# The weighted sums of an attention stage: one fp32 product per block in place of two float16 products

## The chip, the core and the metric

The kernel runs on one core of a Trainium2 chip. The metric is the device time of one execution in microseconds (us); lower is better. The core's engines are named as the profile names them: PE is the tensor engine, PEld its weight loads, DVE the vector engine, ACT the scalar engine, POOL the GpSimd engine, SP the queue that issues most DMAs. Work goes to each engine as a queue in program order.

## What is computed

One layer of a streaming encoder for 1024 tokens of width 1024: an input projection, three groups of heads (stick-breaking attention, a matrix-memory group, a gated group), an output projection, a mixture of 32 experts and a final gate. The change lies in the stick-breaking attention: 6 heads of width 64, blocks of 128 queries.

```python
def stick_breaking_attention(q, k, v):
    for n in range(S // 128):
        t0, kend = n * 128, n * 128 + 128
        z = einsum('bthd,bshd->bhts', q[:, t0:kend], k[:, :kend]) * scale
        log_1m = where(mask, -softplus(z), 0.0)
        after = cumsum(log_1m, axis=3, reverse=True) - log_1m
        a = where(mask, exp(log_sigmoid(z) + after), 0.0)
        outs.append(einsum('bhts,bshd->bthd', a, v[:, :kend]))   # the weighted sums
```

## The kernel before

Float32 results are made from float16 products: a number is split into a high float16 part and a low one (the rest), and a product is the sum of two or three float16 products. `split` (L138 to L140) makes the two parts: ACT copies the high part, DVE subtracts it and writes the low one. `mm3` (L142 to L145) is the three-product form of the projections.

**First part (up to about 106 us).** The input is normalised and turned, and the values are projected into `V`, which holds for each of 8 token blocks and 6 heads a high and a low float16 part of 64 columns beside each other. `values_out` (L364) writes it with `split`.

**The attention stage (about 106 to 400 us).** A hand-written order of slots: 48 steps, one per head and query block; head after head, and in each head the query blocks in the order 0, 7, 1, 6, 2, 5, 3, 4, so that short and long steps alternate. A step with query block i has i+1 blocks of 128 keys; over all steps that is 6 x 36 = 216 blocks. Each slot s runs one stage of several steps and, in between, half-groups of the remaining input projections on PE (`todo`), and side work of the gated and matrix-memory groups on DVE, ACT and POOL (`advance`). The stages of one step, in the slots in which they come:

- `scores` (slot s): PE multiplies queries and keys into a score bank of PSUM.
- `sigmoids` (s+1): ACT writes two sigmoids of the scores, `rest` and `a`.
- `products` (s+2): DVE scans `rest` backwards (L666), POOL multiplies it into `a` (L667). `a` is float32.
- `turned` (s+3): PE transposes each 128x128 block of `a` into one of two PSUM banks, "5" and "6" (L676).
- `high` and `low` (s+4): ACT copies the transposed weights as float16 (`ah`, L683); later in the slot DVE subtracts `ah` from the same PSUM bank and writes the rest as float16 (`al`, L689). A bank is free again when both have read it.
- `values` (s+5): for each block PE multiplies `ah` with high and low values side by side (128 columns, L695) and `al` with the high values (64 columns, L697), all summed in PSUM bank "7", of which there is one.
- `finish` (s+6): DVE adds the two halves of that bank into `ya` (L701). It is the first attention work of its slot on DVE; `values` of the step behind it waits until it has emptied bank "7".

The lines of a slot:

```python
            stage(s - 6, "finish")
            stage(s - 4, "high")
            stage(s - 1, "sigmoids")
            stage(s - 2, "products")
            stage(s - 4, "low")
            advance()
            # half a group of projections on PE, then:
            stage(s - 5, "values")
            # the rest of the slot's projections, then turned (s - 3) and scores (s)
```

**Behind the stage** come the chunks of the matrix memory, the output projection, the router and the experts, whose weights are loaded on SP once the arena that held the turned input is free, which is when the last projection of the stage (`pvb`) has read it.

Of the kernel before, what the change touches and what calls it, by code (L numbers as in the profile page):

```python
# [10 lines left out]
F32 = mybir.dt.float32  # L11
F16 = mybir.dt.float16
I32 = mybir.dt.int32
AF = mybir.ActivationFunctionType
OP = mybir.AluOpType
AX = mybir.AxisListType
# [3 lines left out]
P = 128  # L20
S = 1024
D = 1024
NT = S // P
# [3 lines left out]
ISW = 1.0 / SW  # L27
HA = 6
DA = 64
WA = HA * DA  # L30
# [64 lines left out]
def hybrid_kernel(ctx, tc, x, p, norm1_g, w_in, conv_w, conv_b, igate_b, fgate_b, mnorm_g, sb_out_g,  # L95
# [3 lines left out]
    nc = tc.nc  # L99
    dbg = dbg or {}  # L100

    def pool(c, name, bufs=1, side="left", space=None):
        kw = {"space": space} if space is not None else {"side": side, "reuse_waits": "tile"}
        return c.enter_context(tc.tile_pool(name=name, bufs=bufs, **kw))
# [8 lines left out]
    def bank(which, name, dt=F32, n=512):  # L113
        i = turn.get(which, 0)
        turn[which] = i + 1
        b = which[i % len(which)]
        return ps.tile([P, n], dt, tag="b" + b, name=name)
# [5 lines left out]
    def rows(src, n):  # L123
        return bass.AP(tensor=src.tensor, offset=src.offset, ap=[[0, P], [1, n]])
# [8 lines left out]
    def rnorm(src, n, name, tag):  # L133
        ms = small.tile([P, 1], F32, name=name, tag=tag + "m")
        nc.scalar.activation(jk[:, :n], src, AF.Square, accum_out=ms)
        return rsq(ms, 1, n, name, tag)

    def split(hi, lo, src, scale):  # L138
        nc.scalar.activation(hi, src, AF.Copy, scale=scale)  # L139
        nc.vector.scalar_tensor_tensor(lo, src, scale, hi, op0=OP.mult, op1=OP.subtract)  # L140
# [140 lines left out]
    ya = yap.tile([P, NT, WA], F32, name="ya")  # L281
# [9 lines left out]
    qkp = pool(cA, "qkp", 1, "right")  # L291
    at = pool(cA, "at", 2, "right")
    vp = pool(cA, "vp", 1, "right")
    V = vp.tile([P, NT, HA, 2, DA], F16, name="V")

    rests = {w: vp.tile([P, w + 1], F32, name=f"rest{w}") for w in (512, S)}
    for w in rests:
# [34 lines left out]
    with ExitStack() as cx:  # L332
        xp = pool(cx, "xp", 3, "right")
        g1 = xp.tile([P, D], F32, name="g1", bufs=1)
        vrow = xp.tile([64, P], F32, name="vrow", bufs=1)
        nc.vector.memset(vrow, 0.0)
        xs, rs = {}, {}

        def load(t):
            xs[t] = xp.tile([P, D], F32, name=f"x{t}", tag="x")  # L340
            nc.sync.dma_start(xs[t], x[0, t * P:(t + 1) * P, :])

        def root(t):
            rs[t] = rnorm(xs[t], D, f"r1_{t}", "n1")

        def norm(t):
            nc.vector.scalar_tensor_tensor(xs[t], xs[t], rs[t], g1, op0=OP.mult, op1=OP.mult)

        def turned(t):
            sl = slice(t * P, t * P + P)  # L350
            pts = []
            for k0 in (0, 4):
                pt = bank("56", f"pt{t}{k0}")
                for k in range(4):
                    nc.tensor.transpose(pt[:, k * P:(k + 1) * P], xs[t][:, (k0 + k) * P:(k0 + k + 1) * P], ident)
                pts.append((k0, pt.rearrange("p (k t) -> p k t", t=P)))
            for k0, pt in pts:
                split(hTh[:, k0:k0 + 4, sl], hTl[:, k0:k0 + 4, sl], pt, 1.0)

        def values(t):  # L360
            *_, pz = projN(f"pv{t}", WV, WA, t)
            return pz

        def values_out(t, pz):  # L364
            split(V[:, t, :, 0, :], V[:, t, :, 1, :], pz[:, :WA].rearrange("p (h d) -> p h d", d=DA), ISW)

        loads = [(vrow[16:40], conv_w[0].rearrange("j (k c) -> (j k) c", c=P)),
                 (vrow[40:46], conv_b[0].rearrange("(k c) -> k c", c=P)), (vrow[46:50], sgu_b[0]),
                 (gy[:, 0:WA], rows(sb_out_g, WA)), (gy[:, WA:WA + WM], rows(mnorm_g, WM)),
                 (gy[:, WA + WM:], rows(sgu_out_g, WU)),  # L370
                 (lgb[:, 0], rows(sgu_ln_g, WU)), (lgb[:, 1], rows(sgu_ln_b, WU))]

        def others_turned():
            pv = bank("56", "pvec")
            nc.tensor.transpose(pv[:, :64], vrow, ident[:64, :64])
            nc.vector.tensor_copy(vec, pv[:, :64])
            pt = bank("56", "psw")
            for g in range(NG):
                nc.tensor.transpose(pt[:, g * P:(g + 1) * P], sw[:, g, :], ident)
            nc.vector.tensor_copy(swT, pt.rearrange("p (g t) -> p g t", t=P))  # L380

        sw = xp.tile([P, NG, P], F32, name="sw", bufs=1)
        load(0)
        nc.scalar.dma_start(g1, rows(norm1_g, D))
        with tc.manual_schedule(engines=FOUR):
            awake(48)
            WV = load_w("wv", [(CVA, WA)], "wst4")
            load(1)
            root(0)
            norm(0)  # L390
            turned(0)
            for _ in split_w(WV):
                pass
            load(2)
            root(1)
            norm(1)
            W0 = load_w("w0", [(CQA, P), (CKA, P)], "wst4")
            sp = split_w(W0)
            for t in range(NT):
                if t + 2 < NT:  # L400
                    root(t + 2)
                pz = values(t)
                if t + 1 < NT:
                    turned(t + 1)
                if t + 2 < NT:
                    norm(t + 2)
                values_out(t, pz)
                if t + 3 < NT:
                    load(t + 3)
                for _ in range(2 if t == 2 else t < 2):  # L410
                    next(sp)
                if 0 < t < 5:
                    if t == 1:
                        nc.gpsimd.dma_start(vrow[50:58], ple_norm_g[0].rearrange("(k c) -> k c", c=P))
                    for o, src in loads[2 * t - 2:2 * t]:
                        nc.gpsimd.dma_start(o, src)
                if t == 3:
                    nc.gpsimd.dma_start(sw, sgu_w[0].rearrange("g t s -> t g s"))
                    nc.vector.memset(sw[0:64, :, 64:128], 0.0)
                    for _ in sp:  # L420
                        pass
                if t == 6:
                    others_turned()
                if t % 4 == 3:
                    for mms, then in proj_qk(0, W0, QKS[0], t // 4):
                        *_, pz = mms
                        for _ in then(pz):
                            pass
# [204 lines left out]
    class Step:  # L633
# [42 lines left out]
                    nc.tensor.transpose(pt[:, b * P:(b + 1) * P], self.a[:, (s0 + b) * P:(s0 + b + 1) * P], ident)  # L676
                self.t.append((m, pt))

        def high(self):
            self.hl = []  # L680
            for s, (m, pt) in enumerate(self.t):
                ah = at.tile([P, 512], F16, name=f"ah{self.h}{self.i}{s}", tag="ah", bufs=3)
                nc.scalar.activation(ah[:, :m * P], pt[:, :m * P], AF.Copy)  # L683
                self.hl.append(ah)

        def low(self):
            for s, (m, pt) in enumerate(self.t):
                al = at.tile([P, 512], F16, name=f"al{self.h}{self.i}{s}", tag="al", bufs=3)
                nc.vector.tensor_tensor(al[:, :m * P], pt[:, :m * P], self.hl[s][:, :m * P], op=OP.subtract)  # L689
                self.hl[s] = [(self.hl[s][:, b * P:(b + 1) * P], al[:, b * P:(b + 1) * P]) for b in range(m)]  # L690

        def values(self):
            self.pa = bank("7", f"av{self.h}{self.i}")[:, :P].rearrange("p (l d) -> p l d", l=2)
            for sb, (ah, al) in enumerate(sum(self.hl, [])):
                nc.tensor.matmul(self.pa.rearrange("p l d -> p (l d)"), ah,  # L695
                                 V[:, sb, self.h].rearrange("p l d -> p (l d)"), start=(sb == 0), stop=False)
                nc.tensor.matmul(self.pa[:, 0, :], al, V[:, sb, self.h, 0, :], start=False, stop=(sb == self.i))  # L697

        def finish(self):
            h, i = self.h, self.i  # L700
            nc.vector.tensor_reduce(ya[:, i, h * DA:(h + 1) * DA], self.pa.rearrange("p l d -> p d l"),  # L701
                                    axis=AX.X, op=OP.add)
            if h == HA - 1:
                side.append(self.norm())

# [353 lines left out]
    with tc.manual_schedule(engines=FOUR):  # L1059
# [5 lines left out]
        def stage(s, *fns):  # L1065
            if 0 <= s < NS:
                for f in fns:
                    getattr(steps[s], f)()

        m2, wo = None, w_out_all()  # L1070
        for s in range(NSLOT + 2):
# [22 lines left out]
            fresh.clear()  # L1094
            advance(quick)
            stage(s - 6, "finish")
            stage(s - 4, "high")
            stage(s - 1, "sigmoids")
            stage(s - 2, "products")
            stage(s - 4, "low")  # L1100
            advance()
            want = min(NJ, NJ * (s + 1) // NSLOT)
            if done < want:
# [825 lines left out]
```

## Time and profile before

| | us |
|---|---|
| device time, median of 3 runs (lowest to highest) | 1066.91 (1065.41 to 1067.37) |
| profiled execution, its own time | 1063.69 |
| profiled execution, span from first to last instruction | 1061.8 |
| PE busy in the span | 931.5 (88%) |
| DVE busy | 741.1 (70%) |
| ACT busy | 574.9 (54%) |
| POOL busy | 425.5 (40%) |

The span is the stretch between the first and the last instruction; the profiled execution's own time is 1.9 us more, and 3.2 us under the median. Busy shares are means over stages with different limits, so the stage of the change is read by itself. The duration shown for a matmul reaches to its modelled end, and matmuls overlap in the pipeline; what a chain of matmuls costs is read from start to start.

### The profile page before, as it was taken

Reading aid. Unit: us, or ns where it says so; the run is one execution under the profiler, and the core shown is the slowest. Engines: PE = TensorE matmul, PEld = TensorE weight load, DVE = VectorE, ACT = ScalarE, POOL = GpSimd, SP = SyncE. Lnnn points to the kernel's source line nnn. Section 1 sums busy time; section 2 is a strip of 40 time slices with the busy share of each in tenths; the row PEclk is TensorE's granted clock in tenths of the full one; section 3 lists DMA queues with packets and bytes.
Section 4 is the critical chain, followed back from the end, with each engine's and each line's share of the span. In section 5 each row is a group of like instructions: output and inputs, shape, how many; then the busy total and the mean of one; then the engine's idle time right before and its main releaser. Section 6 shows DMA issues by size and latency. Waiting matters only on the chain. (4 is left out here: it accounts for less than half of the span.)

```text
span 1061.8 us, 15986 instructions
## 1 busy us (share of the span) xinstructions
PE 931.5 (88%) x5927; PEld 538.3 (51%) x5928; DVE 741.1 (70%) x1259; ACT 574.9 (54%) x937; POOL 425.5 (40%) x383
## 2 busy tenths in 40 slices
PE   7899989988999878998887659998899899999795
PEld 4457855544665455555444434543454454445343
DVE  4454549999957965578888649897677777686333
ACT  4344555535557543333333358997676767585422
POOL 2101214565542453132333637844355445561431
PEclk8999989999999997999988789999999999999898
DMA  6411122112320277955358589999989898896330
GB/s 219 130 43 32 38 55 56 35 63 79 112 66 18 90 221 199 297 176 172 104 179 278 203 278 299 284 324 319 295 271 329 253 328 278 295 311 205 81 86 40
DMA packets 128465, 189.54 MB, mean 179 GB/s; under 512 B 13505, under 2 KB 104223, under 8 KB 128384
## 3 DMA queue, kind: packets, MB, share of 16 engines
q1 hardware_dynamic: 113376, 154.40, 45.0%
q0 software_dynamic: 14864, 33.57, 11.6%
q8 instruction: 47, 0.77, 0.3%
q10 hardware_dynamic: 144, 0.52, 0.1%
q14 instruction: 34, 0.28, 0.1%
HBM read 166.01 MB, written 37.31 MB: 191 GB/s over the span
## 5 line engine op out<-in xcount | busy, mean ns | idle before, releaser
L667 POOL TENSOR_TENSOR a<-a,rest 128x128 f32<-128x128 f32 (+7 forms) x48 | 60.7, 1264 | 169.9 <-DVE rest L666 129.0
L1269 POOL DMA_INDIRECT h2s<-yo,tabs x32 | 72.0, 2251 | 72.2 <-issue 25.2
L143 PE MATMUL pg<-arena,xT 128*128 128x512 f16 x256 | 97.8, 382 | 0.7 <-ACT xT L1231 0.7
L145 PE MATMUL pg<-arena,xT 128*128 128x512 f16 x256 | 97.6, 381 | 0.0
L144 PE MATMUL pg<-arena,xT 128*128 128x512 f16 x256 | 97.6, 381 | 0.0
L140 DVE SCALAR_TENSOR_TENSOR arena<-arena 128x2048 f16<-128x2048 f32 (+1 forms) x39 | 81.2, 2096 | 18.4 <-ACT arena L139 18.4
L666 DVE TENSOR_TENSOR_SCAN rest<-rest,one 128x128 f32<-128x128 f32 (+7 forms) x48 | 73.8, 1538 | 7.0 <-ACT rest L659 6.7
L140 DVE SCALAR_TENSOR_TENSOR arena<-ws,arena 128x2048 f16<-128x2048 f32 x29 | 66.0, 2289 | 16.7 <-ACT arena L139 16.6
L145 PEld LDWEIGHTS <-arena 128*128 128x128 f16 x516 | 51.8, 100 | 50.2 <-DVE arena L251 6.5
L144 PEld LDWEIGHTS <-arena 128*128 128x128 f16 x516 | 51.7, 100 | 39.1 <-issue 10.9
L143 PEld LDWEIGHTS <-arena 128*128 128x128 f16 x516 | 52.3, 101 | 37.1 <-issue 4.9
L139 ACT ACTIVATE arena<-arena 128x2048 f16<-128x2048 f32 (+1 forms) x39 | 67.1, 1738 | 0.4 <-DMA arena<-in_w_up_dram 0.4
L139 ACT ACTIVATE arena<-ws 128x2048 f16<-128x2048 f32 x29 | 55.3, 1925 | 2.6 <-DMA ws<-in_w_up_dram 2.6
L683 ACT ACTIVATE ah<-at 128x512 f16<-128x512 f32 (+3 forms) x72 | 32.6, 488 | 37.1 <-PE at L676 36.6
L144 PE MATMUL pd<-dl,hT 128*128 128x512 f16 x120 | 47.6, 397 | 5.2 <-DVE dl L140 5.1
L143 PE MATMUL pd<-dh,hT 128*128 128x512 f16 x120 | 47.6, 397 | 3.4 <-ACT yo L1266 3.3
L143 PE MATMUL po<-woh,yT 128*128 128x512 f16 x128 | 50.3, 393 | 0.0
L144 PE MATMUL po<-wol,yT 128*128 128x512 f16 x128 | 50.3, 393 | 0.0
L145 PE MATMUL po<-woh,yT 128*128 128x512 f16 x128 | 49.9, 390 | 0.0
L689 DVE TENSOR_TENSOR al<-at,ah 128x512 f16<-128x512 f32 (+3 forms) x72 | 36.9, 540 | 17.9 <-ACT ah L683 17.9
L140 DVE SCALAR_TENSOR_TENSOR dl<-arena,dh 128x2048 f16<-128x2048 f32 x17 | 38.9, 2289 | 13.9 <-ACT dh L139 13.9
L145 PE MATMUL pd<-dh,hT 128*128 128x512 f16 x120 | 47.3, 394 | 0.0
(661 smaller groups left out, 2715.3 us busy)
## 6 DMA issues: line engine op xcount, KB each, us to landing
arena<-in_w_down_dram SPq DMA_DIRECT2D x19, 1024.0 KB, 11.8
arena<-in_w_up_dram SPq DMA_DIRECT2D x18, 1024.0 KB, 8.0
arena<-in_w_gate_dram SPq DMA_DIRECT2D x17, 1024.0 KB, 9.4
ws<-in_w_gate_dram SPq DMA_DIRECT2D x14, 1024.0 KB, 10.2
ws<-in_w_up_dram SPq DMA_DIRECT2D x13, 1024.0 KB, 12.9
ws<-in_w_down_dram SPq DMA_DIRECT2D x12, 1024.0 KB, 8.1
arena<-in_w_in_dram SPq DMA_DIRECT2D x16, 384.0 KB, 3.1
x<-in_x_dram SPq DMA_DIRECT2D x8, 512.0 KB, 6.3
```

What stands on the lines that cost most here:

```text
L139: nc.scalar.activation(hi, src, AF.Copy, scale=scale)
L140: nc.vector.scalar_tensor_tensor(lo, src, scale, hi, op0=OP.mult, op1=OP.subtract)
L143: nc.tensor.matmul(o, a[0], w[0], start=first, stop=False)
L144: nc.tensor.matmul(o, a[0], w[1], start=False, stop=False)
L145: nc.tensor.matmul(o, a[1], w[0], start=False, stop=last)
L666: nc.vector.tensor_tensor_scan(back, back, one1.to_broadcast([P, n]), 1.0, op0=OP.mult, op1=OP.mult)
L667: nc.gpsimd.tensor_tensor(self.a[:, :n], self.a[:, :n], self.rest[:, w - n + 1:w + 1], op=OP.mult)
L683: nc.scalar.activation(ah[:, :m * P], pt[:, :m * P], AF.Copy)
L689: nc.vector.tensor_tensor(al[:, :m * P], pt[:, :m * P], self.hl[s][:, :m * P], op=OP.subtract)
L1269: return nc.gpsimd.indirect_dma_start(out=h2s, out_offset=bass.IndirectOffsetOnAxis(ap=self.tb[:, 1:2], axis=0), in_=self.yo, in_offset=No ...
```

## The change

The weights and the values stay in float32. `V` becomes one float32 tile of the same number of bytes, written by ACT alone. `high` becomes `copied`, which writes the transposed weights as float32 (`aT`); `low` is gone. `values` is one float32 matmul of 64 columns per block in place of two float16 matmuls of 128 and 64 columns, and `finish` is a copy in place of a sum of two halves.

```diff
-    V = vp.tile([P, NT, HA, 2, DA], F16, name="V")
+    V = vp.tile([P, NT, HA, DA], F32, name="V")
...
         def values_out(t, pz):
-            split(V[:, t, :, 0, :], V[:, t, :, 1, :], pz[:, :WA].rearrange("p (h d) -> p h d", d=DA), ISW)
+            nc.scalar.activation(V[:, t], pz[:, :WA].rearrange("p (h d) -> p h d", d=DA), AF.Copy, scale=ISW)
...
-        def high(self):
-            self.hl = []
+        def copied(self):
+            self.aT = []
             for s, (m, pt) in enumerate(self.t):
-                ah = at.tile([P, 512], F16, name=f"ah{self.h}{self.i}{s}", tag="ah", bufs=3)
-                nc.scalar.activation(ah[:, :m * P], pt[:, :m * P], AF.Copy)
-                self.hl.append(ah)
-
-        def low(self):
-            for s, (m, pt) in enumerate(self.t):
-                al = at.tile([P, 512], F16, name=f"al{self.h}{self.i}{s}", tag="al", bufs=3)
-                nc.vector.tensor_tensor(al[:, :m * P], pt[:, :m * P], self.hl[s][:, :m * P], op=OP.subtract)
-                self.hl[s] = [(self.hl[s][:, b * P:(b + 1) * P], al[:, b * P:(b + 1) * P]) for b in range(m)]
+                aT = at.tile([P, 512], F32, name=f"aT{self.h}{self.i}{s}", tag="aT", bufs=3)
+                nc.scalar.activation(aT[:, :m * P], pt[:, :m * P], AF.Copy)
+                self.aT += [aT[:, b * P:(b + 1) * P] for b in range(m)]

         def values(self):
-            self.pa = bank("7", f"av{self.h}{self.i}")[:, :P].rearrange("p (l d) -> p l d", l=2)
-            for sb, (ah, al) in enumerate(sum(self.hl, [])):
-                nc.tensor.matmul(self.pa.rearrange("p l d -> p (l d)"), ah,
-                                 V[:, sb, self.h].rearrange("p l d -> p (l d)"), start=(sb == 0), stop=False)
-                nc.tensor.matmul(self.pa[:, 0, :], al, V[:, sb, self.h, 0, :], start=False, stop=(sb == self.i))
+            self.pa = bank("7", f"av{self.h}{self.i}")[:, :DA]
+            for sb, aT in enumerate(self.aT):
+                nc.tensor.matmul(self.pa, aT, V[:, sb, self.h], start=(sb == 0), stop=(sb == self.i))

         def finish(self):
             h, i = self.h, self.i
-            nc.vector.tensor_reduce(ya[:, i, h * DA:(h + 1) * DA], self.pa.rearrange("p l d -> p d l"),
-                                    axis=AX.X, op=OP.add)
+            nc.vector.tensor_copy(ya[:, i, h * DA:(h + 1) * DA], self.pa)
...
             stage(s - 6, "finish")
-            stage(s - 4, "high")
+            stage(s - 4, "copied")
             stage(s - 1, "sigmoids")
             stage(s - 2, "products")
-            stage(s - 4, "low")
             advance()
```

## Rows read from the trace of the kernel before

**Rows 1.** The page's line of busy time: for each engine busy us, share of the span, instructions.

```profile
PE 931.5 (88%) x5927; PEld 538.3 (51%) x5928; DVE 741.1 (70%) x1259; ACT 574.9 (54%) x937; POOL 425.5 (40%) x383
```

**Rows 2.** The attention stage in seven stretches: from and to, length, then busy us and instructions of PE, PEld, DVE, ACT and POOL, the granted clock of PE as a share of full speed, the DMA share and GB/s.

```profile
106.00:148.50 42.50, 42.50 (x387) 34.18 (x385) 20.47 (x30) 24.17 (x50) 9.00 (x7) 1.00 0.21 53
148.50:161.00 12.50, 8.74 (x43) 4.46 (x42) 5.24 (x16) 6.89 (x14) 1.66 (x2) 0.73 0.10 23
161.00:196.00 35.00, 33.93 (x235) 20.21 (x234) 32.37 (x83) 19.18 (x45) 18.18 (x17) 1.00 0.18 46
196.00:270.50 74.50, 64.73 (x412) 37.33 (x410) 72.90 (x149) 35.13 (x77) 42.27 (x34) 0.95 0.22 68
270.50:352.00 81.50, 81.50 (x597) 50.19 (x596) 62.61 (x105) 49.69 (x105) 34.17 (x30) 1.00 0.20 64
352.00:372.00 20.00, 15.28 (x108) 9.12 (x107) 19.82 (x22) 9.77 (x22) 7.64 (x6) 1.00 0.26 92
372.00:399.00 27.00, 19.10 (x153) 13.47 (x153) 18.76 (x29) 13.67 (x28) 13.43 (x16) 0.90 0.79 226
```

**Rows 3.** PE's waits between 105 and 400 us: who waited, for whom, us in total, times, the longest.

```profile
PE av L695 <- DVE ya L701: 16.7, 10, 3.8
PE at L676 <- DVE al L689: 4.8, 3, 2.7
PE pvb L143 <- ACT arena L519: 4.1, 1, 4.1
PE pc L145 <- DVE arena L251: 1.1, 1, 1.1
```

**Rows 4.** PE by line and shape: the two float16 products of the weighted sums, and the product of the gated group (`sgu`), whose operands have the shapes and the type of the changed product; out and in, columns, count, busy us, mean ns, idle before and its releaser. The first two stand 216 times in the program and 216 times in the trace, the third 32 times in the program and 64 times in the trace.

```profile
L695 PE MATMUL av<-V,ah 128*128 128x128 f16 x216 | 25.7, 224 | 16.7 <-DVE ya L701 16.7
L697 PE MATMUL av<-V,al 128*128 128x64 f16 x216 | 24.5, 197 | 0.0
L465 PE MATMUL pm<-arena,wol 128*128 128x64 f32 x64 | 8.5, 276 | 0.8 <-DVE st L451 0.6 <-DVE yc L470 0.2
```

**Rows 5.** PE in order of time around one `values` step of 6 blocks (12 matmuls; the first is shown, and the transposes that follow the last) and one `sgu` group of 4 float32 products: start us, us, engine, line, operands, count.

```profile
192.96 0.22 PE L695 MATMUL av<-V,ah 128*128 128x128 f16 x1
...
193.47 0.74 PE L676 MATMUL at<-ident,a 128*128 128x128 f32 x5
...
194.32 1.06 PE L465 MATMUL pm<-arena,wol 128*128 128x64 f32 x8
195.22 0.38 PE L143 MATMUL pc<-arena 128*128 128x512 f16 x1
```

**Rows 6.** PE in order of time at four float32 products of 97 columns behind the stage.

```profile
419.38 1.06 PE L797 MATMUL pi<-Cst,qk 96*128 96x97 f32 x8
420.28 0.33 PE L143 MATMUL pvb<-arena 128*128 128x384 f16 x1
```

**Rows 7.** Line 695 alone in the stretches of rows 2: from and to, length, busy us of PE and of PEld with their counts (one per block of keys), clock, DMA share, GB/s.

```profile
106.00:148.50 42.50, 3.58 (x31) 2.80 (x31) 1.00 0.21 53
148.50:161.00 12.50, 0.91 (x5) 0.71 (x5) 0.73 0.10 23
161.00:196.00 35.00, 3.10 (x27) 2.44 (x27) 1.00 0.18 46
196.00:270.50 74.50, 5.74 (x45) 4.49 (x45) 0.95 0.22 68
270.50:352.00 81.50, 8.27 (x72) 6.61 (x73) 1.00 0.20 64
352.00:372.00 20.00, 1.33 (x11) 0.99 (x11) 1.00 0.26 92
372.00:399.00 27.00, 2.79 (x25) 2.15 (x24) 0.90 0.79 226
```

**Rows 8.** Groups of DVE and ACT that the change removes or alters, and their nearest kin: out and in, shapes, count, busy us, mean ns, idle before and its releaser.

```profile
L689 DVE TENSOR_TENSOR al<-at,ah 128x512 f16<-128x512 f32 (+3 forms) x72 | 36.9, 540 | 17.9 <-ACT ah L683 17.9
L701 DVE TENSOR_REDUCE ya<-av 128x64 f32<-128x128 f32 x48 | 13.6, 284 | 8.8 <-PE av L697 8.6
L616 DVE COPY wc<-grc 128x128 f32<-128x128 f32 x1 | 0.3, 286 | 0.0
L140 DVE SCALAR_TENSOR_TENSOR V<-pv,V 128x384 f16<-128x384 f32 x8 | 4.4, 553 | 0.1
L683 ACT ACTIVATE ah<-at 128x512 f16<-128x512 f32 x36 | 20.8, 596 | 27.2 <-PE at L676 26.9
L661 ACT ACTIVATE a<-z 128x512 f32<-128x512 f32 x36 | 21.2, 611 | 0.0
```

**Rows 9.** Line 689 alone in two of the stretches: from and to, length, busy us of DVE with the count, clock, DMA share, GB/s.

```profile
196.00:270.50 74.50, 7.22 (x15) 0.95 0.22 68
352.00:372.00 20.00, 2.79 (x5) 1.00 0.26 92
```

**Rows 10.** ACT and DVE in order of time around the long wait of the second stretch.

```profile
144.73 3.62 ACT L483 ACTIVATE woh<-woh 128x4096 f32<-128x4096 f32 x1
150.90 1.41 DVE L308 SCALAR_TENSOR_TENSOR wol<-pq,wol 64x512 f16<-64x512 f32 x2 [7.28 <-ACT wol L306]
152.34 0.29 DVE L701 TENSOR_REDUCE ya<-av 128x64 f32<-128x128 f32 x1
```

**Rows 11.** SP's queue: the issue of the first load of expert weights.

```profile
422.54 1.79 SPq L1190 DMA_DIRECT2D arena<-in_w_gate_dram  x1
```

## The prediction, made from the trace of the kernel before

> **What bounds the kernel now.** I read the busy line first: PE is the fullest engine with 931.5 us of 1061.8, DVE the next with 741.1 [rows 1]. That is a mean; the change lives in the attention stage, so I cut the stage into stretches by which engine has no idle time [rows 2]. The reader is to see two regimes. In 106 to 148.5 and in 270.5 to 352 PE is busy all the time, 42.5 of 42.5 and 81.5 of 81.5 us at full clock, while DVE has 22.0 and 18.9 us to spare: PE is the pace. In 196 to 270.5 and 352 to 372 it is the other way: DVE is busy 72.9 of 74.5 and 19.8 of 20 us, and PE idles 9.8 and 4.7 us. The stretches between are mixed: 161 to 196 (PE idles 1.1 us), 148.5 to 161 (3.8 us) and the tail from 372 (7.9 us). All idle time of PE in the seven stretches is 27.2 us of 293. Then I read PE's waits [rows 3]: 16.7 us until DVE's `finish` (L701) empties bank "7", 4.8 us until DVE's `low` frees a transpose bank. So PE waits for DVE, but not because these two operations are long: they stand in a DVE queue that is full.
>
> **The price on PE.** A `values` step of 6 blocks runs from 192.96 to the next work at 193.47 us [rows 5]: 0.51 / 6 = 0.085 us per block, for a 128- and a 64-column float16 product. The float32 product that replaces them is in the trace already, in the same shapes: a 128x128 weight against 64 columns, in the gated group. Four of them run as 8 records from 194.32 to 195.22 us [rows 5], 0.225 us per product; the trace has two records for each product of the program [rows 4]. So a block costs 0.14 us more, and 216 blocks 30.2 us.
>
> Two things could make one doubt that price. By columns alone the new product moves two passes of 64 against 128 + 64 before, so it would cost 0.085 x 128/192 = 0.057 us, a gain of 216 x 0.028 = 6 us. The rows deny that: four products of 97 columns take 419.38 to 420.28, again 0.225 us each [rows 6], so the time does not hang on columns but on what else each record brings, its weights. The Trainium skill (TensorE: Matmul & The Clock Gate, Weight-path perf modes) says that the fast weight load is off for FP32 weights; the trace agrees, with about 0.11 us per float32 record at 64 and at 97 columns. The Trainium skill (FP8 and Floating Point Precision, TensorE Precision Notes) says that a true FP32 product is four passes through the array; at 0.11 us each that would be 0.45 us a block and about 79 us in all as an estimate, but the rows show two records and the 0.225 us holds whatever is in them.
>
> **What is taken off DVE.** `low` goes: 72 instructions, 36.9 us [rows 8]. `finish` falls from 0.284 us to a 64-column copy; the nearest copy, of 128 columns, took 0.286 [rows 8], so 0 is the one bound, and half of it (0.14 us) the other; I take 0.06 us each, 3 us in all. Where DVE is the pace this is time; where PE is, it is nothing.
>
> **What costs nothing.** ACT writes float32 in place of float16: 128x512 took 611 ns from PSUM to float32 and 596 ns to float16 [rows 8], 72 x 0.015 = 1 us at most, on an engine that is half idle. The tiles take the same bytes, and `aT` has three buffers as `ah` had. `V` loses its low part, 8 x 0.553 = 4.4 us of DVE [rows 8], before 106 us; no wait of the stage's PE names it, so I count 0 (bound: 4.4 us gained).
>
> **The sum by stretches**, with the blocks of each [rows 7] at 0.14 us:
>
> - 106 to 148.5: 31 blocks, no idle time on PE: +4.3.
> - 148.5 to 161: 5 blocks, +0.7. PE waits 3.8 us for an L701 that stands behind DVE's L308, which waited 7.28 us for ACT behind a 3.62 us activation [rows 10]. The change shortens nothing there, but 4 blocks' extra work before it (0.6) hides in the wait: 0. Bounds: +0.7, and -3.1 if the wait vanished.
> - 161 to 196: 27 blocks, +3.8, less the 1.1 us that PE waits for a DVE split (L251) that now comes earlier: +2.7.
> - 196 to 270.5: 45 blocks, +6.3. DVE is the pace and loses 7.2 us [rows 9] and 11 x 0.06 = 0.7: 65.0 us of work are left of 72.9. PE has 64.7 + 6.3 = 71.0 us [rows 2]. So PE becomes the pace: -3.5. The granted clock of 0.95 here [rows 2] means that for a tenth of the stretch PE ran at 1.2 GHz and not 2.4, in and behind its waits; if these go, up to 74.5 x 0.05 = 3.7 us more come back: -7.2. I take -5.5, nearer to the middle, since the engines alternate slot by slot and each slot is as long as its slower one.
> - 270.5 to 352: 72 blocks, no idle time: +10.1.
> - 352 to 372: 11 blocks, +1.5. DVE 19.8 - 2.8 - 0.2 = 16.8; PE 15.3 + 1.5 = 16.8: -3.2 at best; I take -2.7.
> - 372 to 399: 25 blocks, +3.5, against 7.9 us of idle time, of which 4.1 are behind ACT's L519 [rows 3], not behind DVE; the 2.7 us wait for `low` goes. At best 3.5 - 7.9 = -4.4, at worst +3.5; I take -0.5.
>
> Sum: 4.3 + 0 + 2.7 - 5.5 + 10.1 - 2.7 - 0.5 = +8.4 us. Nothing behind the stage makes up for it: the first expert weights are asked for at 422.5 us [rows 11], behind the last projection, so that the rest moves with the stage. Against the profiled execution this is 1063.7 + 8.4 = 1072.1; the median of the runs shown lies 3.2 us higher, and the forecast is for such a median: 1066.9 + 8.4, or about 1075 us.
>
> **The rivals.** Changes under 0.2% (2.1 us) are about what a measurement of this kernel cannot tell from none.
>
> - *PE pays in two regimes, DVE's relief gives part back* (forecast): 1075, own range 1069 to 1083. Chance 0.62.
> - *The waits do not go*: what holds PE in 196 to 270.5 and 352 to 372 is the slot's chain (scan, POOL, transposes), not the load of DVE. Then little of the 30.2 us is hidden: with the returns of the fourth and sixth stretch halved against their best, 4.3 + 0.7 + 3.8 - 1.8 + 10.1 - 1.6 + 1.7 = +17.2, with none +30.2, so 1084 to 1097. For it: L701 itself is short. Against: DVE has 1.6 us of idle time in 74.5. Chance 0.12.
> - *DVE is the bound and its relief wins*: slots in which PE waits lose all their waits and PE comes back to full clock. The idle time alone is 27.2 us and leaves +3.0; the slow-clock shares, 12.5 x 0.27 + 74.5 x 0.05 + 27 x 0.10 = 9.8 us, overlap it. It decides once more than 30.2 us return, that is all the waits and a third of the clock: about 1063 us. For it: 21.5 us of waits name DVE. Against: 7.9 of the 27.2 us hang on ACT (rows 3 and 10 show 4.1 and 3.8), which the change does not relieve. Chance 0.13.
> - *The two cancel* within 2.1 us: 28 to 32 us return. 1067. Chance 0.12.
> - *The product is not priced as in the gated group*: 79 us by four passes (1146) or -6 by columns. Denied by rows 5 and 6; chance 0.01.
>
> **Range.** The best values of all stretches give 4.3 - 3.1 + 2.7 - 7.2 + 10.1 - 3.2 - 4.4 = -0.8, or 1066; with the edge of the faster case 1065. Upwards I stop behind the halved returns, 1084, at 1086; about 0.1 is left out on each side. Slower by over 0.2%: 0.62 + 0.12 + 0.01 = 0.75; within: 0.12; faster: 0.13.
>
> **What would show it.** In the profile after, the weighted sums should have 432 records of 64 float32 columns, 0.225 us per block from start to start; the stretch up to the long activation should be some 4 us longer and the one that now is 270.5 to 352 some 10 us, both without idle time on PE; L689 gone and DVE's busy time down by some 44 us (36.9 + 4.4 + 3); waits of PE for L701 down from 16.7 to under 8 us, and the clock of the fourth stretch near 1.00. I am wrong if float32 records follow each other faster than 0.11 us between other matmuls, if PE's waits in the fourth and sixth stretch stay, or if the stage ends earlier than now because DVE carried it also where PE has no idle time.

## The result, and the profile of the changed kernel

The changed kernel takes 1072.06 us (median of 5 runs, 1070.01 to 1075.18) beside 1066.91 for the kernel before: a ratio of 1.0066, 95% interval 1.0047 to 1.0084. Measured once more beside the later experiments it is 1070.01 against 1065.22, ratio 1.0054 (1.0030 to 1.0078). The medians put it 5.1 and 4.8 us (0.5%) behind the kernel before, the two ratios 0.5 to 0.7%; the forecast was 8 us. The change is slower, by 5 to 7 us.

The page's line of busy time of the changed kernel, beside [rows 1]:

```profile
PE 959.2 (90%) x5927; PEld 571.7 (53%) x5928; DVE 702.3 (66%) x1179; ACT 575.0 (54%) x937; POOL 439.1 (41%) x383
```

DVE has 80 instructions and 38.8 us less, PE 27.7 us more. PE's count is the same, since each float32 product is two records. PE by line and shape, and DVE's new `finish`, beside [rows 4, 8]:

```profile
L689 PE MATMUL av<-V,aT 128*128 128x64 f32 x432 | 55.5, 275 | 7.7 <-DVE ya L693 7.4
L693 DVE COPY ya<-av 128x64 f32<-128x64 f32 x48 | 10.5, 218 | 32.3 <-PE av L689 32.0
```

Who waits for whom has turned round: PE's waits for `finish` fell from 16.7 us [rows 3] to 7.4, and DVE's waits in front of `finish` rose from 8.8 [rows 8] to 32.3. Experiments 1 and 2 tell which half of the change did that: it is mostly PE's longer work and not DVE's relief.

The stage in the same seven stretches. The cuts are moved with the work: each lies at the same place between two `values` steps as in [rows 2]. The columns are those of [rows 2].

```profile
107.10:153.00 45.90, 45.90 (x385) 38.06 (x384) 13.48 (x19) 24.08 (x50) 9.84 (x7) 1.00 0.16 44
153.00:166.60 13.60, 10.31 (x45) 5.93 (x44) 4.86 (x15) 6.86 (x13) 1.65 (x2) 0.75 0.10 21
166.60:203.90 37.30, 37.30 (x237) 24.18 (x235) 32.98 (x76) 19.28 (x45) 19.36 (x17) 1.00 0.17 43
203.90:273.10 69.20, 66.71 (x410) 41.82 (x409) 65.43 (x133) 34.76 (x77) 42.05 (x34) 1.00 0.25 74
273.10:363.40 90.30, 90.30 (x598) 60.41 (x596) 49.81 (x83) 50.05 (x105) 42.45 (x31) 1.00 0.18 57
363.40:379.30 15.90, 15.90 (x109) 10.67 (x108) 15.72 (x16) 9.27 (x23) 10.57 (x6) 1.00 0.47 115
379.30:405.60 26.30, 22.29 (x160) 16.59 (x160) 17.47 (x25) 14.34 (x29) 13.68 (x16) 1.00 0.75 232
```

The lengths, against those of before, give this table:

| stretch (times of before) | blocks | forecast | measured |
|---|---|---|---|
| 106 to 148.5 | 31 | +4.3 | +3.4 |
| 148.5 to 161 | 5 | 0 | +1.1 |
| 161 to 196 | 27 | +2.7 | +2.3 |
| 196 to 270.5 | 45 | -5.5 | -5.3 |
| 270.5 to 352 | 72 | +10.1 | +8.8 |
| 352 to 372 | 11 | -2.7 | -4.1 |
| 372 to 399 | 25 | -0.5 | -0.7 |
| sum | 216 | +8.4 | +5.5 |

The reader is to see the two regimes side by side. Where PE had no idle time the stretch became longer, and DVE's relief is visible there only as more idle time of DVE: in 270.5 to 352 its busy time fell from 62.6 to 49.8 us and bought nothing. Where DVE had none, the stretch became shorter although PE has more to do in it.

The spans of the two profiles differ by 8.7 us, more than the stage and more than the medians. The first `values` step comes 1.2 us later (111.44 for 110.27 us); in the kernel of experiment 2 below, which is unchanged up to that point, it comes 1.2 us later too, so this is no effect of the change. The rest came behind the stage and is treated in the last section.

### The profile page after: what moved, and what is told of

Same layout as the page of the kernel before. It is cut to its first block, busy times and chain, and to the rows that moved or that the text cites. A ratio compares the mean times of both kernels' runs of the same rounds, so it can differ in the third digit from the quotient of the medians.

```text
span 1070.5 us, 15892 instructions
## 1 busy us (share of the span) xinstructions
PE 959.2 (90%) x5927; PEld 571.7 (53%) x5928; DVE 702.3 (66%) x1179; ACT 575.0 (54%) x937; POOL 439.1 (41%) x383
## 5 line engine op out<-in xcount | busy, mean ns | idle before, releaser
L667 POOL TENSOR_TENSOR a<-a,rest 128x128 f32<-128x128 f32 (+7 forms) x48 | 70.5, 1468 | 170.9 <-DVE rest L666 90.9
L140 DVE SCALAR_TENSOR_TENSOR arena<-arena 128x2048 f16<-128x2048 f32 (+1 forms) x39 | 80.8, 2088 | 18.5 <-ACT arena L139 18.4
L666 DVE TENSOR_TENSOR_SCAN rest<-rest,one 128x128 f32<-128x128 f32 (+7 forms) x48 | 71.8, 1495 | 10.1 <-ACT rest L659 9.9
L689 PEld LDWEIGHTS av<-V,aT 128*128 128x128 f32 x432 | 55.2, 195 | 15.5 <-DVE ya L693 11.8
L689 PE MATMUL av<-V,aT 128*128 128x64 f32 x432 | 55.5, 275 | 7.7 <-DVE ya L693 7.4
L683 ACT ACTIVATE aT<-at 128x512 f32<-128x512 f32 (+3 forms) x72 | 32.7, 489 | 51.0 <-PE at L676 50.3
L143 PE MATMUL pd<-dh,hT 128*128 128x512 f16 x120 | 47.6, 396 | 3.8 <-ACT yo L1256 3.7
```

The source lines that it names most:

```text
L143: nc.tensor.matmul(o, a[0], w[0], start=first, stop=False)
L666: nc.vector.tensor_tensor_scan(back, back, one1.to_broadcast([P, n]), 1.0, op0=OP.mult, op1=OP.mult)
L667: nc.gpsimd.tensor_tensor(self.a[:, :n], self.a[:, :n], self.rest[:, w - n + 1:w + 1], op=OP.mult)
L683: nc.scalar.activation(aT[:, :m * P], pt[:, :m * P], AF.Copy)
L689: nc.tensor.matmul(self.pa, aT, V[:, sb, self.h], start=(sb == 0), stop=(sb == self.i))
```

## The experiments

In all of them "in the stage" means the change in the start of the last `values` step against the kernel before, less the change in the start of the first; for the changed kernel this is 6.6 - 1.2 = 5.4 us, and 5.5 us in its second profile.

**1. The price without the relief.** DVE keeps a pass over each transposed bank.

```diff
+        def low(self):
+            for s, (m, pt) in enumerate(self.t):
+                aT = self.whole[s]
+                nc.vector.tensor_tensor(aT[:, :m * P], pt[:, :m * P], aT[:, :m * P], op=OP.max)
...
             stage(s - 2, "products")
+            stage(s - 4, "low")
```

> The changed kernel, but DVE keeps a pass over every transposed bank in the place where `low` stood: it takes the larger of bank and float32 copy, which are equal, into the copy, so that the result stays and the bank and the copy wait for DVE as they did before. Theory (PE pays everywhere, and DVE's relief gives back what DVE's full queue had cost): the relief is gone, the price stays. Where DVE is the pace the price hides in PE's idle time (the stretches that were 196 to 270.5 and 352 to 399: 0), elsewhere it is paid: about 4 + 1 + 2 + 9 = 16 us over the kernel before, 1083 us, that is 11 slower than the changed kernel (1072). PE's waits for L701's successor are back at about 10 us or more. Rival (the relief of DVE is worth nothing; the waits went because the operands are ready earlier or for another reason): about 1072, as the changed kernel.

Measured: 1079.91 us, ratio 1.0139 (1.0098 to 1.0180); 14.3 us in the stage, 8.9 more than the changed kernel. Its stretches that answer to 196 to 270.5 and 270.5 to 352 (columns as before):

```profile
203.70:279.00 75.30, 70.92 (x410) 43.60 (x409) 71.77 (x148) 34.95 (x77) 42.23 (x34) 0.93 0.22 68
279.00:369.30 90.30, 90.30 (x598) 60.40 (x596) 62.97 (x106) 50.15 (x105) 34.15 (x30) 1.00 0.18 58
```

The second is 90.3 us long, to the tenth that of the changed kernel, though DVE is busy 63.0 us in it and not 49.8: where PE is the pace DVE's relief is worth nothing. The first stayed at 75.3 us where the changed kernel has 69.2: the price hides there (+0.8 us for 45 blocks), and the gain is the relief alone. The rival, that the relief is worth nothing, falls. PE's waits between 105 and 410 us (here L699 is `finish` and L690 the pass that was kept):

```profile
PE av L695 <- DVE ya L699: 9.1, 7, 3.2
PE at L676 <- DVE aT L690: 2.7, 2, 1.4
```

About 10 us or more were expected for the first. The two were 16.7 and 4.8 us in the kernel before, so the longer work on PE takes nearly half of these waits by itself, with DVE as full as it was.

**2. The relief without the price.**

```diff
-                al = at.tile([P, 512], F16, name=f"al{self.h}{self.i}{s}", tag="al", bufs=3)
-                nc.vector.tensor_tensor(al[:, :m * P], pt[:, :m * P], self.hl[s][:, :m * P], op=OP.subtract)
-                self.hl[s] = [(self.hl[s][:, b * P:(b + 1) * P], al[:, b * P:(b + 1) * P]) for b in range(m)]
+                self.hl[s] = [(self.hl[s][:, b * P:(b + 1) * P], self.hl[s][:, b * P:(b + 1) * P]) for b in range(m)]
```

> The kernel before without `low`: the second float16 product of each block takes the high part again in place of the low one (so the weighted sums are wrong in the low part), same shapes and counts on PE, 72 DVE instructions (36.9 us) less. Theory: PE's work is unchanged, so only the stretches in which DVE is the pace get shorter: 196 to 270.5 by about 7 to 8, 352 to 372 by 3, the tail and 161 to 196 by 1 each: 1054 us (1050 to 1058). Stretches 106 to 148.5 and 270.5 to 352 stay within 0.5 us. Rival (PE's waits are the chain of the slot, not the load of DVE): 1065 or more.

The second float16 product takes the high part a second time here, so that the weighted sums come out about twice as large, not only wrong in their low part as that text says; the same holds for the heads that experiments 5 and 6 change. PE's instructions keep their number and shapes.

Measured: 1054.91 us, ratio 0.9900 (0.9867 to 0.9932); -11.2 us in the stage. The stretch of 196 to 270.5 and PE's waits in it:

```profile
195.50:264.70 69.20, 61.51 (x411) 35.73 (x410) 66.73 (x133) 35.12 (x77) 42.11 (x34) 1.00 0.24 74
```

```profile
PE av L693 <- DVE ya L699: 6.3, 5, 1.9
```

It is 69.2 us long, as in the changed kernel, whose PE has 45 x 0.126 = 6 us more to do in it. So PE's work alone does not set this length; DVE, busy 66.7 of 69.2 us, is nearest to doing so even after the relief, and PE still waits 6.3 us for its `finish` (L699 here), where it waited 6.9 us before. The relief gives 5.3 us and not 7 to 8. The PE-paced stretches did not move: between the steps at 271.45 and 347.59 us of before the shift stays at -5.84 us (-7.02 in the stage).

Where the gain comes from is seen between the first and the last `values` step, first in the kernel before, then in this one, with PE's waits for `finish` in this one between 105 and 390 us:

```profile
110.27:394.64 284.37, 260.92 (x1879) 164.65 (x1877) 227.97 (x422) 153.69 (x324) 121.79 (x106) 0.97 0.25 73
111.45:384.57 273.12, 254.65 (x1878) 162.07 (x1876) 204.63 (x353) 153.51 (x324) 132.79 (x106) 0.99 0.25 75
```

```profile
PE av L693 <- DVE ya L699: 16.5, 10, 3.8
```

PE's waits for `finish` are what they were, 16.5 us in ten waits for 16.7 in ten: relieving DVE does not remove them. PE's idle time falls by 5.0 us (23.4 to 18.5), and the waits for `low`, 4.8 us [rows 3], are gone. The other 6.3 us are PE doing the same work in less busy time, at a granted clock of 0.99 for 0.97. Put together with experiment 1: the relief alone gives -11.2 us in the stage, the price alone +14.3, both +5.4. With the relief in place the price therefore adds 16.7 of its 27.2 us, and the rest fills idle time of PE.

**3 and 4. The change in one place alone.** The form is chosen by head; the six heads are worked off one after the other, so that a choice of heads is a choice of place.

```diff
+    FULL = (2, 5)          # experiment 4: (0, 1, 3, 4)
+    V32 = V.rearrange("p t h l d -> p t h (l d)").bitcast(F32)
...
+                if h in FULL:
+                    nc.tensor.matmul(self.pa, ah, V32[:, sb, h], start=(sb == 0), stop=(sb == i))
+                    continue
```

> The float32 form for heads 2 and 5 alone, whose `values` lie in the two stretches in which DVE is the pace (213 to 271 and 352 to 399 us of the kernel before); the other heads keep two float16 parts. The value columns are written in four pieces in the first part. Theory: the gains stay (-5 in the first of these, -4 in the second, up to -1 in the tail), the price of the other stretches is not paid: -9, 1058 us (1055 to 1062). Rival (cost and gain are not tied to the place; a third of the blocks carries a third of the change): +1.7, 1068.6.

> The complement: the float32 form for heads 0, 1, 3 and 4, two float16 parts for heads 2 and 5. Theory: price without most of the gain: +4 up to 148.5, +1 up to 161, +2 up to 196, +9 from 270.5 to 352: +15, 1082 us (1078 to 1085). Rival (two thirds of the change): +3.4, 1070.

Measured: heads 2 and 5 1061.51 us, ratio 0.9973 (0.9936 to 1.0010), -5.6 us in the stage, with 1.0 us more in the first part than the other kernels for the four pieces of the value columns. Heads 0, 1, 3 and 4: 1077.29 us, ratio 1.0106 (1.0069 to 1.0142), +10.1 us in the stage. The kernel with heads 0, 1, 3 and 4 writes its value columns in four pieces too and comes 1.8 us later into the stage than the others. The first interval touches 1, so that this gain rests on the stage; 0.9 of its 5.6 us lie ahead of head 2, where experiment 6 has them without any change. The place decides: a third of the blocks brings a gain, the other two thirds nearly twice the loss of the whole change. Their sum, +4.5 us, is near the 5.4 of the whole. But both fell short of what was expected (-9 and +15), and in part for one reason. The stretch of head 2, from its first step at 213.10 to the first of head 3 at 271.45 us, gained 2.5 us with the relief in it (5 expected) and 2.5 us without it (0 expected); with both it gains 5.2. The two kernels in that stretch, heads 2 and 5 first (58.35 us before):

```profile
214.38:270.23 55.85, 50.70 (x318) 32.16 (x317) 54.51 (x105) 26.99 (x60) 31.48 (x27) 1.00 0.26 82
223.10:278.96 55.86, 47.95 (x318) 28.12 (x316) 54.46 (x112) 27.29 (x60) 29.12 (x25) 0.97 0.24 72
```

Relief ahead of head 2 pays in head 2. This asked for the next run. The rest of the two misses lies behind 352 us: there the first kernel gained 2.0 us (4 to 5 expected) and the second 3.1 (nothing expected).

**5. Is DVE's backlog carried on?** The subtraction is left out in head 1 alone.

```diff
+                if self.h in (1,):
+                    al = self.hl[s]
+                else:
                     nc.vector.tensor_tensor(al[:, :m * P], pt[:, :m * P], self.hl[s][:, :m * P], op=OP.subtract)
```

> The kernel before without the subtraction in head 1 alone (its steps write the second product from the high part again, so head 1 is wrong in the low part). Head 1 stands in front of the stretch in which DVE is the pace. Theory A (DVE's backlog is carried on: what is taken off before the stretch is given back in it): about -1 up to the first step of head 2, and another -2 to -3 within head 2, whose own steps are unchanged; -3 in all. Theory B (a relief counts only in its own slots): -1 before head 2 and 0 behind.

Measured: 1061.83 us, ratio 0.9967 (0.9946 to 0.9988); -4.7 us in the stage, -3.1 of them up to the first step of head 3. First this kernel, then the kernel before, in three stretches cut at the same places in the work: most of head 1, from there to the first step of head 2, and head 2.

```profile
162.30:196.30 34.00, 33.48 (x233) 20.00 (x232) 32.38 (x74) 18.62 (x43) 18.28 (x17) 1.00 0.19 47
196.30:212.80 16.50, 16.50 (x104) 9.11 (x103) 16.29 (x34) 8.35 (x20) 11.66 (x9) 1.00 0.18 49
212.80:269.70 56.90, 47.77 (x318) 28.20 (x317) 55.74 (x113) 27.35 (x60) 30.64 (x26) 0.97 0.25 79
```

```profile
161.00:195.50 34.50, 33.43 (x233) 19.98 (x232) 31.87 (x81) 18.68 (x43) 18.18 (x17) 1.00 0.19 47
195.50:213.10 17.60, 16.66 (x103) 9.09 (x102) 17.39 (x37) 8.39 (x19) 10.40 (x8) 1.00 0.17 45
213.10:271.40 58.30, 49.48 (x317) 29.01 (x316) 56.91 (x114) 27.24 (x60) 31.86 (x27) 0.94 0.25 77
```

The first two stretches are shorter by 1.6 us together. The third is shorter by 1.4 us, though its own work on DVE is unchanged (113 and 114 instructions), and the granted clock of PE is 0.97 there and was 0.94. Theory B, that a relief counts only in its own slots, does not fit; theory A does, with half the size expected of the second part. This is one profile of each kernel, and another 1.6 us came behind 377 us, where the two kernels do the same work, so the 1.4 us by themselves would be thin; the 2.5 us of experiment 4, with head 2 as before, say the same.

**6. The relief of heads 2 and 5 without its price.**

```diff
+                if self.h in (2, 5):
+                    al = self.hl[s]
+                else:
                     nc.vector.tensor_tensor(al[:, :m * P], pt[:, :m * P], self.hl[s][:, :m * P], op=OP.subtract)
```

> The kernel before without the subtraction in heads 2 and 5 alone (wrong in the low part of these heads), PE's work unchanged: the relief of the first hybrid without its price. If the price hides in PE's idle time there, this is no faster than that hybrid apart from its 1 us in the first part: -0.4 to -0.5%. If the price is paid even there: 72 blocks by 0.126 us = 9 us better than that hybrid, -1.1%.

Measured: 1058.60 us, ratio 0.9945 (0.9928 to 0.9962); -7.1 us in the stage. The hybrid with the price is at -5.3 to -5.6 there (experiments 7 and 3). So by the profiles, of the 9 us that the 72 blocks cost PE, 1.5 to 1.8 us are paid in these stretches and the rest hides. The medians are further apart: this kernel is 4.6 us below experiment 7, so that by them half of the 9 us would be paid. Head 2 by itself is the clearest:

```profile
213.54:269.10 55.56, 46.49 (x318) 27.33 (x317) 54.52 (x105) 27.30 (x60) 31.88 (x27) 1.00 0.26 80
```

It is 55.56 us long without the price and 55.85 with it, with DVE busy 54.5 us in both: the 4.5 us of head 2's 36 blocks hide almost whole, and what is paid is paid in head 5 and the tail.

Not all of the 7.1 us is the relief. Between the `values` steps at 152.68 and 162.07 us of before, this kernel is still the kernel before. First that one, then this one:

```profile
152.68:162.07 9.39, 9.39 (x45) 4.85 (x45) 4.58 (x15) 3.84 (x8) 1.66 (x2) 0.72 0.07 17
154.03:162.50 8.47, 8.47 (x45) 4.60 (x45) 4.58 (x15) 3.84 (x8) 1.65 (x2) 0.80 0.08 18
```

The 0.9 us is a granted clock of 0.80 for 0.72 in this execution. Both hybrids are 0.9 to 1.0 us shorter there too, ahead of their float32 heads, so that from head 2 on the gains are 6.2 us without the price and 4.3 to 4.6 with it.

**7. A hybrid with two pieces.** The float32 heads stand at the end of the tile, so that the value columns need one `split` and one copy.

```diff
+    PLACE = (0, 1, 4, 2, 3, 5)
...
+            src = pz[:, :WA].rearrange("p (a b d) -> p a b d", a=2, d=DA)
+            v = V[:, t, 0:4].rearrange("p (a b) l d -> p a b l d", a=2)
+            split(v[:, :, :, 0, :], v[:, :, :, 1, :], src[:, :, 0:2], ISW)
+            nc.scalar.activation(V32[:, t, 4:6], src[:, :, 2], AF.Copy, scale=ISW)
```

> As the kernel with heads 2 and 5 in float32, but the value columns are written in two pieces per token block in place of four (the float32 heads stand at the end of the tile), since that kernel came 1 us later into the stage. Theory: 1 us better than that one, about -0.4% against the kernel before (-3 to -6 us), and 12 to 15 us better than the changed kernel. Rival (that hybrid's gain was chance): within 0.2% of the kernel before.

Measured: 1063.15 us, ratio 0.9984 (0.9966 to 1.0003). The first part no longer costs 1.0 us (the stage begins 1.2 us later than in the profile of the kernel before, as in the kernels that are unchanged there), and the stage gains 5.3 us as it did; the medians differ by 2.1 us only, and the interval touches 1. It was expected 3 to 6 us below the kernel before and 12 to 15 below the changed one. It is 7 us better than the changed kernel, and its 0.16% lies within the 0.2% that the rival gave for no gain at all: the stage is shorter in both profiles of a hybrid, but a gain in the whole time is not shown.

**8. The changed kernel again.**

> The changed kernel once more, beside the others on this chip, with a second profile: +0.5 to +0.9% against the kernel before. The two complementary hybrids gave -0.27 and +1.06%; if the parts add up, their sum, +0.8%.

Measured: ratio 1.0054, as told above. Its second profile repeats the stage of the first within 0.2 us in each of the three stretches that carry the argument:

```profile
204.80:274.20 69.40, 66.93 (x411) 41.97 (x410) 65.62 (x133) 35.07 (x78) 42.05 (x34) 1.00 0.24 74
274.20:364.50 90.30, 90.30 (x598) 60.34 (x596) 49.83 (x82) 50.01 (x105) 42.42 (x31) 1.00 0.18 57
364.50:380.40 15.90, 15.90 (x109) 10.69 (x107) 15.73 (x16) 9.28 (x23) 10.57 (x6) 1.00 0.48 115
```

The sum of the two hybrids, -0.27 + 1.06 = +0.8%, lies at the upper edge of its interval.

## Why the prediction was right, step by step

**The price on PE**: right in kind, 10% too high. A step of 6 blocks in the changed kernel:

```profile
200.00 1.45 PE L689 MATMUL av<-V,aT 128*128 128x64 f32 x12
201.29 0.72 PE L676 MATMUL at<-ident,a 128*128 128x128 f32 x5
```

1.29 us for 12 records: eleven distances of 0.1115 us and 0.06 for the last, where the group that I read the price from paid 0.12 behind its last record. At full clock the weighted sums of all 48 steps take 45.5 us from start to start and took 18.3: 27.2 us, 0.126 a block, and not 30.2. That is what is missing in the first and the fifth stretch (+3.4 for 4.3, +8.8 for 10.1). Both doubts about the price were settled as the rows had it: neither columns nor a number of passes, but 0.11 us for each of two records. That it is the weights that cost this time was argued and not tried.

**148.5 to 161**: forecast 0, measured +1.1. The wait stayed, as I had said, since ACT's long activation holds it (PE waits 3.3 us there and waited 3.8). What I left out is that PE comes out of this wait at 1.2 GHz: the granted clock of the stretch is 0.75, and the step of 5 blocks behind the wait, 0.77 us before, takes 2.19; at full clock such a step takes 1.06. A price read at 2.4 GHz must be doubled where the clock is down. The stretch also differs by 0.9 us between executions of kernels that are alike in it (experiment 6), so the 1.1 us is no exact figure.

**196 to 270.5**: -5.3 for -5.5, the value between my two floors, and the clock came back to 1.00 as said. That the number fits so well is luck, for the reason was not the one I gave. I made PE the new pace (71.0 us of work, 67.3 with the clock); experiment 2 has the same 69.2 us with 6 us less on PE, so PE alone is not it. DVE's floor of 65.0 us of work was right (65.4 measured), and some 4 us of idle time stay on it between the slots; what exactly sets these 4 us was not tried. And of the 5.2 us that head 2 gains, 2.5 came with relief given ahead of head 2 alone (experiment 4; 1.4 in experiment 5). I counted each relief in its own slots and had no term for that; how much of it comes from ahead of the cut at 196 was not tried.

**352 to 372**: -4.1 for -2.7, better than the floor that I had set (-3.2), which again was taken from the stretch alone; DVE's instructions in it fell from 22 to 16, one more than the 5 of `low`; that DVE gets there with less left over, as in head 2, would fit, but was not tried here. **The tail** (-0.7 for -0.5) and **161 to 196** (+2.3 for +2.7) are as said.

**DVE's relief**: `low` is gone and `finish` takes 218 ns for 284, as estimated (0.06 each). The sum, 38.8 us, is 5 us short of the 44 that I named, in part because other work on DVE became dearer: 4.0 us of it are the 32 small operations below. **PE's waits for `finish`** fell to 7.4 us, under the 8 that I named, but not as I thought. I had them go because DVE is relieved; with the relief alone they stay at 16.5 us (experiment 2), and it is the price that fills them. **ACT** is unchanged, 575.0 for 574.9 us. **Behind the stage** nothing made up for it: the medians moved by what the stage moved. **The sum**: the misses by stretch are -0.9, +1.1, -0.4, +0.2, -1.3, -1.4 and -0.2 us, together -2.9; the price read too high is most of it, and the sign and the size of the whole rest on the two regimes, which the experiments bear out.

**The rivals.** That the waits do not go: right in that PE's waits for `finish` stay when DVE is relieved (what holds them was not tried), wrong about the time. With the relief alone PE's idle time in the fourth stretch falls only from 9.8 us [rows 2] to 7.7, yet the stretch is 5.3 us shorter, and the price hides in what is left: 2.5 us of idle time in the changed kernel. That the two cancel: the stage is 5.4 and 5.5 us longer, and both intervals lie above 1.002. That the relief wins: it would have had to return more than the price; experiment 2 shows all that the relief can return when PE pays nothing, 11 us, against 27 of price, of which experiment 1 shows 14 to be paid.

## What to carry to other kernels

Cut the stage into stretches by which engine has no idle time before adding up: the same edit cost 8.8 us in one of these stretches and gave 5.3 in the one before it, and the mean of busy shares tells neither. A change that moves work from one engine to another is worth trying where the receiving engine idles; applied there alone it was 7 us better than everywhere, though not clearly better than not at all. Relief of a full queue can pay later than where it is given, and not at its full size: the subtraction left out in head 1, about 6 us of DVE (a sixth of 36.9), gave back 1.6 us before head 2 and 1.4 in it. A wait that names an engine need not go when that engine is relieved: ask for the two halves of a change in runs of their own.

## What the runs showed of the hardware that I had not expected

**Beside a relieved DVE, POOL and small DVE operations take longer.** The same 48 products of POOL (L667) and the same 32 small DVE operations (L457) became slower in the changed kernel, 60.7 to 70.5 us and 16.5 to 20.5 us. It is the relief that does it: with the relief alone (experiment 2) they take 69.9 and 21.6 us, with the price alone (experiment 1) 60.7 and 17.1. POOL's group on the two pages, before and after:

```profile
L667 POOL TENSOR_TENSOR a<-a,rest 128x128 f32<-128x128 f32 (+7 forms) x48 | 60.7, 1264 | 169.9 <-DVE rest L666 129.0
```

```profile
L667 POOL TENSOR_TENSOR a<-a,rest 128x128 f32<-128x128 f32 (+7 forms) x48 | 70.5, 1468 | 170.9 <-DVE rest L666 90.9
```

DVE's L457 stands in eight groups of four. The shortest, median and longest operation in ns of two groups before, and of the same two after:

```profile
L457 DVE TENSOR_SCALAR arena<-woh,mv,rs4r x4: 303/675/1810, 212.7 to 215.6; 128x64 f32<-128x64 f32 x4
L457 DVE TENSOR_SCALAR arena<-woh,mv,rs2r x4: 302/304/641, 186.8 to 187.8; 128x64 f32<-128x64 f32 x4
```

```profile
L457 DVE TENSOR_SCALAR arena<-woh,mv,rs4r x4: 303/304/1349, 219.2 to 220.9; 128x64 f32<-128x64 f32 x4
L457 DVE TENSOR_SCALAR arena<-woh,mv,rs2r x4: 301/302/1343, 191.2 to 192.9; 128x64 f32<-128x64 f32 x4
```

One and the same operation takes either about 0.3 us or 0.64 to 2.04 us, and those that are held up are not more after the change, 8 of 32 for 9, but longer. The first group shown ran from 212.68 to 215.82 us before; its two long operations ended at 213.73 and 215.45 us, right behind these two of POOL, which end at 213.68 and 215.40:

```profile
210.25 3.43 POOL L549 TENSOR_TENSOR ca<-ca,cs 128x1024 f32<-128x1024 f32 x1
213.63 1.77 POOL L667 TENSOR_TENSOR a<-a,rest 128x896 f32<-128x896 f32 x1
```

The Trainium skill (SBUF — State Buffer, SBUF: two separate sides) says that GpSimd and DVE operations of certain forms take a shared pair of ports as an exclusive lock, for the whole instruction. The trace agrees as to the ends: in all ten profiles together 87 of these operations were long (641 to 2151 ns), and every one ended 48 to 58 ns behind the end of one of these two kinds of POOL operation. Overlap as such is not enough, since others took 0.3 us with POOL busy all through. That it is this lock is argued and not shown, as no run here took the overlap away by itself, and so is why relief makes these longer still.

**The clock behind the stage differs from one execution to the next.** The same kernel, from the same place behind the last `values` step to the first product of the output projection, in its two profiles:

```profile
405.60:437.40 31.80, 25.38 (x144) 18.43 (x143) 17.61 (x45) 10.84 (x31) 9.77 (x20) 0.77 0.75 228
```

```profile
406.70:434.20 27.50, 22.23 (x143) 16.26 (x142) 16.83 (x43) 10.08 (x29) 8.92 (x20) 0.88 0.80 242
```

31.8 us at a granted clock of 0.77 against 27.5 at 0.88; the kernel before took 32.2 at 0.77 in its profile. Waits of PE for ACT and DVE stand there, of 2.5, 1.8 and 2.2 us in the first and 3.3, 1.6 and 0.5 us in the second; the granted clock falls to 1.2 GHz three times in the first and once in the second. That is 4.3 us, nearly the size of the effect, between two executions of one program: a single profile's span would have put the change at 8.7 or at 2.8 us, and the stage by itself (5.4 and 5.5) and the medians (5.1 and 4.8) repeat.
